# A two-layer hybrid mixer: another opening of the first layer, and three changes to its planner

## Chip, cores and metric

The kernel runs on one core of a Trainium2 chip. The metric is the device time of one execution in microseconds (us). Times of engines and transfers come from one profiled execution.

## What is computed

Two layers, each a modulated RMSNorm, one projection into four token mixers, gates, and an output projection with a residual. There are 512 tokens and 256 context tokens of 1024 channels. Of the reference, this is what the change touches:

```python
def rmsnorm(x, gain):
    xf = x.astype(jnp.float32)
    y = xf * lax.rsqrt(jnp.mean(xf * xf, axis=-1, keepdims=True) + EPS)
    return (y * gain.astype(jnp.float32)).astype(x.dtype)
...
        shift, scale, gate = jnp.split((silu_c @ w_mod[l] + b_mod[l])[:, None, :], 3, axis=-1)
        shift_c, scale_c, gate_c = jnp.split(silu_cc @ w_mod[l] + b_mod[l], 3)
        h = rmsnorm(x, norm_gain[l]) * (1.0 + scale) + shift
        hc = rmsnorm(xc, norm_gain[l]) * (1.0 + scale_c) + shift_c
        za, zb, zh, zf, zg = jnp.split(h @ w_in[l], SPLIT_IDX, axis=-1)
```

## The kernel before

The kernel is written as calls on a recording object, `Program`. `record` (line 199) turns each call into an operation with a cost and a rank; `order` (line 255) then plans all five engines with these costs and fixes one order of instructions for each engine and for the transfer queue of SP. Among the operations that an engine could start at the same planned time, the one of lowest rank comes first. The rank is the place in the program, less `AHEAD` = 400 for the loads and the splitting of weights. On the chip each engine takes its instructions strictly in that order, and each waits on semaphores for what it needs.

Every large product is made of three: an operand is split into a rounded part and a rest, `hi` and `lo` (`split`, line 485: ScalarE, called ACT, rounds; VectorE, called DVE, subtracts), and TensorE, called PE, adds hi·hi, hi·lo and lo·hi in PSUM. Weights arrive as raw blocks `wraw` of 128 x 1024 through SP's queue and are split into `wh` and `wl` in two halves of 512 (`Weights`, line 490). Working tiles are taken from 29 shared slots of 128 x 768, all named `u` in the profile; a tile that takes over a slot waits for the last reader of the one before it.

The stage in question is `opening` (line 653), ahead of the first projection. It loads the 768 tokens as eight blocks `x[j, u]` (3 x 128 tokens, 256 channels each); squares each block on ACT, sums the squares on DVE, and computes the reciprocal root `r` by a chain of small DVE operations (`rstd`, line 744, and `rsqrt`, line 468), once for each half `u` of the tokens; multiplies the blocks by `r` on DVE; transposes them on PE, six blocks of 128 x 128 for each of the eight channel groups `k`, and evicts the result with ACT as `xT[k]`. Meanwhile eight modulation weight chunks arrive, 1 MB each; PE multiplies each with the conditioning (`mod_rows`, tile `psg<-u,cst`), ACT evicts the row (`mrow`), PE turns it into columns (`columns`, `psg<-kc,mrow`) and DVE puts two of them together as scale and shift (`mod_columns`, tile `modc`). Of eight chunks, two are needed for each pair of channel groups. Then

```python
for c, n0, n1 in ((0, 0, NX), (1, NX, NT)):
    ts(xT[k][:, n0:n1], xT[k][:, n0:n1], mc[:, 0, k, c:c + 1], mc[:, 1, k, c:c + 1])
split(hi_t[:, k, :], lo_t[:, k, :], xT[k])
```

makes `h_hi` and `h_lo`, and the first projection (`psw<-h_hi,wh`, the forget gates of the recurrent mixer) starts accumulating as the channel groups come.

The masks of the recurrent mixer are loaded as int32 into slots and cast to int8 on DVE (`load_masks`, called in `hg_mix`).

Of the kernel before, what the change touches and what calls it, by code (L numbers as in the profile page):

```python
# [163 lines left out]
WINDOW = 300  # L164
AHEAD = 400
BEHIND = 0
ATOM = 4
LAT = {"tensor": 0.2, "vector": 0.13, "scalar": 0.15, "gpsimd": 0.13}


class Program:
# [27 lines left out]
    def record(self, engine, method, args, kw):  # L199
        writes = [v for v in [args[0], kw.get("accum_out")] if isinstance(v, View)]  # L200
        reads = [v for v in list(args[1:]) + [v for k, v in kw.items() if k != "accum_out"] if isinstance(v, View)]
        dma = method == "dma_start"
        last = self.last
        if engine == "tensor" and last is not None and last.engine == "tensor" and last.tiles[0] is args[0].tile:
            op = last
        else:
            op = Op(len(self.ops), engine)
            op.rank -= self.ahead
            self.ops.append(op)
        self.last = op  # L210
        op.calls.append((engine, method, args, kw))
        for v in writes + reads:
            if v.tile not in op.tiles:
                op.tiles.append(v.tile)
                v.tile.touch += 1
        for v, w in [(v, False) for v in reads] + [(v, True) for v in writes]:
            r = v.region()
            log = v.tile.log
            for q, x, xw in log:
                if (w or xw) and x is not op and _overlap(r, q):  # L220
                    op.preds.add(x)
            if w:
                log[:] = [e for e in log if not _covers(r, e[0])]
            log.append((r, op, w))
        op.cost += self.price(engine, method, args, kw)
        op.latency = 2.0 if dma else LAT[engine]
        if dma:
            op.transfer = math.prod(args[0].shape) * 4 / 3e5

    def price(self, engine, method, args, kw):  # L230
        o = args[0]
# [23 lines left out]
    def order(self):  # L255
# [15 lines left out]
        for t in span:  # L271
            k = t.space, t.tag
            if k not in free:
                free[k] = [0.0] * t.bufs
                assert live[k].max() <= t.bufs, (k, live[k].max(), int(live[k].argmax()))
        made, done, out, moved = set(), set(), [], 0.0
        oldest = 0
        while len(out) < len(ops):
            while oldest < len(ops) and ops[oldest] in done:
# [78 lines left out]
def tile_hybrid_mixers(ctx, tc, io, out, dump=None):  # L358
# [65 lines left out]
    csel = kc[:, KC_SEL:KC_SEL + 2]  # L424
    rsel = [kc[:, KC_SEL + 2 + w:KC_SEL + 3 + w].to_broadcast([P, P]) for w in range(2)]
    masks = cpool.tile([P, len(LEVELS), P], I8, name="masks")

    hi_t = hpool.tile([P, 8, NT], F32R, tag="hhi", name="h_hi")
    lo_t = hpool.tile([P, 8, NT], F32R, tag="hlo", name="h_lo")

    def load_masks():
        for a, b in ((0, 4), (4, len(LEVELS))):
            mraw = slot([P, b - a, P], I32)
            nc.gpsimd.dma_start(mraw, io["masks"][:, a:b, :])
            nc.vector.tensor_copy(masks[:, a:b, :], mraw)


    sides, done, flags = [], set(), set()
# [53 lines left out]
    class Weights:  # L492
# [3 lines left out]
        def __init__(self, plan):  # L496
            self.plan = list(plan)
            self.raw, self.ready, self.work = [], [], None
            self.held = self.current = 0

        def fetch(self):
            while self.plan and len(self.raw) + bool(self.work) < RAW_BUFS:
                t = wpool.tile([P, 1024], F32, tag="wraw", bufs=RAW_BUFS, name=nm("wraw"))
                nc.ahead = AHEAD
                nc.sync.dma_start(t, self.plan.pop(0))
                nc.ahead = 0
                self.raw.append(t)

        def emit(self):
            if self.work is None:  # L510
                hi, lo = (wpool.tile([P, 1024], F32R, tag=g, bufs=W_BUFS, name=nm(g)) for g in ("wh", "wl"))
                self.work = [hi, lo, self.raw.pop(0), 0]
            hi, lo, raw, a = self.work
            c = slice(a, a + 512)
            nc.ahead = AHEAD
            split(hi[:, c], lo[:, c], raw[:, c])
            nc.ahead = 0
            self.work[3] += 512
            if a + 512 == 1024:
                self.ready.append((hi, lo))  # L520
                self.work = None
                self.fetch()
# [114 lines left out]
        act(rows, ps)  # L637
        return rows

    def columns(tmp, j, rows):  # L640
        ps = psg()[:, 0:4]
        for b in range(2):
            mm(ps[:, 2 * b:2 * b + 2], rows[:, P * b:P * (b + 1)], csel)
        nc.vector.tensor_copy(tmp[:, j // 4, 2 * (j % 4):2 * (j % 4) + 2, :], ps.rearrange("p (k w) -> p k w", w=2))
# [10 lines left out]
    def opening():  # L655
# [3 lines left out]
        tmp = small(32, "mt", 1).rearrange("p (a k w) -> p a k w", a=2, w=2)  # L659
        norm = Norm(None)  # L660
        x = {}
        for u in range(2):
            for j in range(4):
                x[j, u] = slot([P, 3, 256])
                nc.sync.dma_start(x[j, u], io["xin"][384 * u:384 * (u + 1), 256 * j:256 * (j + 1)].rearrange("(t p) d -> p t d", p=P))
        fetch = lambda i: [mod_fetch(io["w_mod"][0, j]) for j in (4 + i, i)]
        w = {0: fetch(0)}
        weights.fetch()
        for u in range(2):
            for j in range(4):  # L670
                sq = slot([P, 3, 256])
                act(sq, x[j, u], AF.Square)
                nc.vector.tensor_reduce(norm.ss[:, 3 * u:3 * u + 3, j], sq, AX.X, ALU.add)
            r = norm.rstd(3 * u, 3 * u + 3, 4)
            for j in range(4):
                tt(x[j, u], x[j, u], r.unsqueeze(2).to_broadcast([P, 3, 256]), ALU.mult)
        w[1] = fetch(1)
        xT = []
        for i in range(4):
            for k in (2 * i, 2 * i + 1):  # L680
                ps = psw()[:, 0:NT]
                for t in range(6):
                    transpose(ps[:, P * t:P * (t + 1)], x[i, t // 3][:, t % 3, P * (k % 2):P * (k % 2 + 1)])
                xT.append(slot())
                act(xT[k], ps)
        for i in range(4):
            for j, wj in zip((4 + i, i), w.pop(i)):
                columns(tmp, j, mod_rows(wj))
            mod_columns(0, mc, tmp, 2 * i, 2 * i + 2)
            for k in (2 * i, 2 * i + 1):  # L690
                for c, n0, n1 in ((0, 0, NX), (1, NX, NT)):
                    ts(xT[k][:, n0:n1], xT[k][:, n0:n1], mc[:, 0, k, c:c + 1], mc[:, 1, k, c:c + 1])
                split(hi_t[:, k, :], lo_t[:, k, :], xT[k])
            if i < 2:
                w[i + 2] = fetch(i + 2)
                for _ in range(4):
                    weights.pump()

    def modulation(l):

# [32 lines left out]
    class Norm:  # L733
# [8 lines left out]
            act(junk, x, AF.Square, accum_out=self.ss[:, t, j:j + 1])  # L742

        def rstd(self, t0, t1, n):
            v = small(3, "sv", 1)
            m = t1 - t0
            nc.vector.tensor_reduce(v[:, 0:m], self.ss[:, t0:t1, 0:n], AX.X, ALU.add)
            ts(v[:, 0:m], v[:, 0:m], 1.0 / D, EPS)
            return rsqrt(v[:, 0:m], m, 3)

        def scale(self, t0, t1, n):

# [505 lines left out]
    def hg_mix(l, z, res):  # L1258
# [1 line left out]
        W = NT if full else NX  # L1260
        nch = W // P
        yield from wait_for((l, "hf", 0))
        if full:
            load_masks()
        fl, om, dl = hg_bounds(l)
        gn = small(64, "hgn", 1)
        nc.gpsimd.dma_start(gn, io["smalls"][l:l + 1, SM_HGG:SM_HGG + 64].partition_broadcast(P).rearrange("p a d -> p (a d)"))
# [345 lines left out]
def _constants():  # L1613
# [13 lines left out]
            kc[r, KC_SEL + w] = 1.0  # L1627
            kc[r, KC_SEL + 2 + w] = 0.5
    i = np.arange(P)
    masks = np.zeros((P, len(LEVELS), P), np.int32)  # L1630
    for n, L in enumerate(LEVELS):
        same = (i[:, None] // (2 * L)) == (i[None, :] // (2 * L))
        masks[:, n] = same & ((i[:, None] // L) != (i[None, :] // L))
# [85 lines left out]
```

## Time and profile before

| what | value |
|---|---|
| median of 3 runs | 1495.21 us (1494.02 to 1495.75) |
| the profiled execution's own time | 1493.43 us |
| its span, first to last instruction | 1491.7 us |
| PE, DVE, ACT busy | 1436.5, 950.8, 627.6 us |

The span leaves 1.7 us of the profiled execution's own time outside. Matmuls overlap, so a row's duration for PE is longer than the step from one to the next, and a busy PE need not be at its peak.

### The profile page before, as it was taken

What the parts mean: (1) busy time and instruction counts of PE and PEld (TensorE: products, weight loads), DVE (VectorE), ACT (ScalarE), POOL (GpSimd) and SP (SyncE); (2) the same over time, 40 slices, a digit from 0 to 9 for tenths busy, and PEclk for the clock granted to TensorE, in tenths of its full rate; (3) what the DMA queues carried; (4) which work ended last, traced back from release to release, by engine and by line L of the source; (5) the groups of instructions that cost most, each with busy time, mean ns of one, the idle gap of its engine ahead of it and who ended that gap; (6) DMA issues with size and microseconds to landing.
All of it is one profiled execution on the core that took longest, in us unless ns stands there. A gap on an engine that the chain in (4) does not pass through costs nothing.

```text
span 1491.7 us, 25385 instructions
## 1 busy us (share of the span) xinstructions
PE 1436.5 (96%) x10068; PEld 1317.4 (88%) x10068; DVE 950.8 (64%) x2058; ACT 627.6 (42%) x1384; POOL 107.2 (7%) x207
## 2 busy tenths in 40 slices
PE   1999999999999999999999999999999999999998
PEld 0899989999999999999999989898888889888788
DVE  5696898677663267633444477889867755674544
ACT  3444353465532245422323354535456633543330
POOL 0000000500000000100000110000130000110000
PEclk9999999999999999999999999999999999999999
DMA  9311101622321135543123321101353222464322
GB/s 349 103 44 57 33 30 60 138 70 97 107 89 57 57 82 169 140 132 123 57 78 101 96 98 57 57 33 58 90 143 88 89 74 88 141 160 160 104 96 78
DMA packets 50598, 144.76 MB, mean 97 GB/s; under 512 B 7280, under 2 KB 12400, under 8 KB 50480
## 3 DMA queue, kind: packets, MB, share of 16 engines
q1 hardware_dynamic: 38336, 112.21, 23.1%
q0 software_dynamic: 12144, 30.93, 8.4%
q8 instruction: 79, 1.29, 0.4%
q14 instruction: 39, 0.32, 0.1%
HBM read 123.98 MB, written 4.19 MB: 86 GB/s over the span
## 4 chain that ended last, share of the span: by engine, by line
PE 86%; DVE 5%; ACT 4%; issue 2%; DMA 2%; SPq 1%; POOL 0%; ACTq 0%; DVEq 0%; POOLq 0%
PE psg L353 70%; PE psw L353 11%; PE pst L353 5%; DVE u L353 4%; ACT u L353 3%; ACT wh L353 1%; DMA u<-u 1%; SPq L353 1%; DVE sm L353 1%; DMA u<-in_w_mod_dram 1%; ACT mth L353 0%; DVE wl L353 0%; DVE nss L353 0%; DVE dd L353 0%; DVE h_lo L353 0%
## 5 line engine op out<-in xcount | busy, mean ns | idle before, releaser
L353 PE MATMUL psg<-h_hi,wh 128*128 128x384 f32 (+2 forms) x1216 | 438.5, 361 | 2.9 <-ACT mth L353 2.8
L353 PE MATMUL psg<-h_hi,wl 128*128 128x384 f32 (+2 forms) x1216 | 428.6, 352 | 0.0
L353 PE MATMUL psg<-h_lo,wh 128*128 128x384 f32 (+2 forms) x1216 | 428.0, 352 | 0.3 <-DVE h_lo L353 0.3
L353 DVE TENSOR_TENSOR wl<-wraw,wh 128x512 fp32r<-128x512 f32 x312 | 201.6, 687 | 186.1 <-ACT wh L353 185.4
L353 ACT ACTIVATE wh<-wraw 128x512 fp32r<-128x512 f32 x312 | 180.6, 625 | 259.3 <-PE psg L353 246.5
L353 PEld LDWEIGHTS psg<-h_hi,wh 128*128 128x128 f32 x1216 | 228.7, 188 | 23.7 <-ACT mth L353 5.7
L353 PEld LDWEIGHTS psg<-h_hi,wl 128*128 128x128 f32 x1216 | 228.5, 188 | 16.0
L353 PEld LDWEIGHTS psg<-h_lo,wh 128*128 128x128 f32 x1216 | 228.9, 188 | 14.5 <-DVE h_lo L353 0.5
L353 PE MATMUL psg<-wh,h_hi 128*128 128x256 f32 x544 | 157.1, 289 | 0.0
L353 PE MATMUL psg<-wl,h_hi 128*128 128x256 f32 x544 | 151.6, 279 | 0.0
L353 PE MATMUL psg<-wh,h_lo 128*128 128x256 f32 x544 | 151.5, 279 | 0.0
L353 PE MATMUL psw<-u,u 64*128 64x128 f32 (+6 forms) x1144 | 135.4, 295 | 8.8 <-ACT u L353 3.1
L353 PEld LDWEIGHTS psw<-u,u 64*128 64x128 f32 (+2 forms) x1144 | 110.8, 188 | 22.0 <-issue 6.0
L353 ACT ACTIVATE u<-psw,sm 128x768 f32<-128x768 f32 (+2 forms) x120 | 90.7, 758 | 77.6 <-DVE sm L353 75.1
L353 DVE SCALAR_TENSOR_TENSOR mth<-mth,psg 128x384 f32<-128x384 f32 (+1 forms) x96 | 57.1, 594 | 87.3 <-ACT mth L353 72.9
L353 ACT ACTIVATE u<-psw 128x768 f32<-128x768 f32 (+10 forms) x208 | 93.8, 472 | 44.2 <-PE psw L353 40.9
L353 PE MATMUL psg<-wh,u 128*128 128x256 f32 x640 | 110.6, 277 | 0.9 <-ACT mth L353 0.9
L353 ACT ACTIVATE mth<-psg 128x384 f32<-128x384 f32 (+1 forms) x120 | 62.3, 520 | 113.2 <-PE psg L353 112.9
L353 PE MATMUL psg<-yg,wh 128*128 128x384 f32 (+1 forms) x384 | 107.1, 360 | 0.0
L353 PEld LDWEIGHTS psg<-wh,h_hi 128*128 128x128 f32 x544 | 102.2, 188 | 3.8
L353 PEld LDWEIGHTS psg<-wl,h_hi 128*128 128x128 f32 x544 | 103.0, 189 | 0.2
L353 PEld LDWEIGHTS psg<-wh,h_lo 128*128 128x128 f32 x544 | 102.3, 188 | 0.0
(134 smaller groups left out, 1960.1 us busy)
## 6 DMA issues: line engine op xcount, KB each, us to landing
wraw<-in_w_merge_dram SPq DMA_DIRECT2D x64, 512.0 KB, 3.5
wraw<-in_w_in_dram SPq DMA_DIRECT2D x60, 512.0 KB, 3.8
u<-in_w_mod_dram SPq DMA_DIRECT2D x32, 384.0 KB, 6.4
wraw<-in_w_up_dram SPq DMA_DIRECT2D x16, 512.0 KB, 3.5
wraw<-in_w_out_dram SPq DMA_DIRECT2D x16, 512.0 KB, 3.8
u<-u POOLq DMA_DIRECT2D x72, 96.0 KB, 2.4
u<-in_w_gate_dram SPq DMA_DIRECT2D x16, 384.0 KB, 6.3
u<-u POOLq DMA_DIRECT2D x24, 192.0 KB, 2.8
```

The costliest lines, as they stand in the source:

```text
L353: getattr(getattr(nc, engine), method)(*map(f, args), **{k: f(v) for k, v in kw.items()})
```

## The change

In `opening`, the token blocks are loaded channel group by channel group, and transposed and evicted unscaled. One chain of roots serves all 768 tokens. Its result is put on the diagonals of six blocks (`dg`) and multiplied by a matrix of ones, so that PE writes `r` as a row over all partitions, evicted as `R`. Then `h = xT * scale * R` is one two-tensor operation on DVE per range of tokens, ACT adds the shift while it rounds (`h_hi`), and a second two-tensor operation on DVE makes `h_lo`. The columns of the modulation use the PSUM buffer `t` in place of one of the three buffers `g`.

The first raw weight blocks lose their early rank during the opening (`rush`). The masks come as int8 straight to their place. In the planner, transfers are costed at 380 bytes per ns in place of 300 and begin at 3.0 us, and an operation other than on PE that reads PSUM has a rank lower by 500.

```diff
+EVICT = 500
...
         dma = method == "dma_start"
+        evict = not dma and engine != "tensor" and any(v.tile.space == "ps" for v in reads)
...
-            op.rank -= self.ahead
+            op.rank -= EVICT if evict else self.ahead
...
-            op.transfer = math.prod(args[0].shape) * 4 / 3e5
+            op.transfer = math.prod(args[0].shape) * 4 / 3.8e5
...
-        made, done, out, moved = set(), set(), [], 0.0
+        made, done, out, moved = set(), set(), [], 3.0
...
+    nc.gpsimd.dma_start(masks, io["masks"])
...
-    def load_masks():
-        for a, b in ((0, 4), (4, len(LEVELS))):
-            mraw = slot([P, b - a, P], I32)
-            nc.gpsimd.dma_start(mraw, io["masks"][:, a:b, :])
-            nc.vector.tensor_copy(masks[:, a:b, :], mraw)
...
-                nc.ahead = AHEAD
+                nc.ahead = self.rush
...
-        for u in range(2):
-            for j in range(4):
+        for j in range(4):
+            for u in range(2):
                 x[j, u] = slot([P, 3, 256])
                 nc.sync.dma_start(x[j, u], io["xin"][384 * u:384 * (u + 1), 256 * j:256 * (j + 1)].rearrange("(t p) d -> p t d", p=P))
...
         weights.fetch()
-        for u in range(2):
-            for j in range(4):
+        w[1] = fetch(1)
+        for j in range(4):
+            for u in range(2):
                 sq = slot([P, 3, 256])
                 act(sq, x[j, u], AF.Square)
                 nc.vector.tensor_reduce(norm.ss[:, 3 * u:3 * u + 3, j], sq, AX.X, ALU.add)
-            r = norm.rstd(3 * u, 3 * u + 3, 4)
-            for j in range(4):
-                tt(x[j, u], x[j, u], r.unsqueeze(2).to_broadcast([P, 3, 256]), ALU.mult)
...
+        for k in range(6):
+            turn(k)
+        r = norm.rstd(0, 6, 4)
+        dg, ones, R = slot([P, 6, P]), slot([P, P]), slot()
+        nc.vector.memset(ones, 1.0)
+        tt(dg, ident.unsqueeze(1).to_broadcast([P, 6, P]), r.unsqueeze(2).to_broadcast([P, 6, P]), ALU.mult)
+        ps = psw()
+        mm(ps[:, 0:512], ones, dg[:, 0:4, :])
+        mm(ps[:, 512:768], ones, dg[:, 4:6, :])
+        act(R, ps[:, 0:NT])
+        for k in (6, 7):
+            turn(k)
...
-                columns(tmp, j, mod_rows(wj))
+                columns(tmp, j, mod_rows(wj), pst()[:, 0:4])
...
-                    ts(xT[k][:, n0:n1], xT[k][:, n0:n1], mc[:, 0, k, c:c + 1], mc[:, 1, k, c:c + 1])
-                split(hi_t[:, k, :], lo_t[:, k, :], xT[k])
+                    h, hi, lo = xT[k][:, n0:n1], hi_t[:, k, n0:n1], lo_t[:, k, n0:n1]
+                    stt(h, h, mc[:, 0, k, c:c + 1], R[:, n0:n1], ALU.mult, ALU.mult)
+                    act(hi, h, AF.Identity, bias=mc[:, 1, k, c:c + 1])
+                    stt(lo, h, mc[:, 1, k, c:c + 1], hi.bitcast(F32), ALU.add, ALU.subtract)
...
+        weights.rush = AHEAD
```

The new `turn(k)` holds the six transposes and the eviction that stood in a loop before. `rstd` and `rsqrt` work on six columns in place of three.

The first place where the order moves is ACT in the opening. Names: `u_176<-u_99` is a square of a token block, `u_305<-psw_290` the eviction of a transposed channel group, `mrow` a modulation row, `wh` the rounding of a raw weight block. Before:

```order
L353 ACTIVATE u_176<-u_99 128x768
L353 ACTIVATE u_185<-u_101 128x768
L353 ACTIVATE u_198<-u_105 128x768
L353 ACTIVATE u_208<-u_107 128x768
L353 ACTIVATE u_228<-u_111 128x768
L353 ACTIVATE mrow_234<-psg_218 128x256
L353 ACTIVATE wh_242<-wraw_131 128x512 x2
L353 ACTIVATE mrow_280<-psg_262 128x256
L353 ACTIVATE u_305<-psw_290 128x768
```

Now:

```order
L355 ACTIVATE u_222<-u_101 128x768
L355 ACTIVATE u_231<-psw_212 128x768
L355 ACTIVATE u_234<-u_103 128x768
L355 ACTIVATE u_246<-psw_224 128x768
L355 ACTIVATE mrow_259<-psg_236 128x256
L355 ACTIVATE u_261<-psw_248 128x768
L355 ACTIVATE u_266<-u_107 128x768
L355 ACTIVATE mrow_282<-psg_268 128x256
L355 ACTIVATE wh_69<-wraw_68 128x512 x2
L355 ACTIVATE wh_297<-wraw_128 128x512 x2
L355 ACTIVATE mrow_341<-psg_323 128x256
L355 ACTIVATE u_359<-psw_346 128x768
```

All eight evictions now stand among the squares; the last square is `u_266<-u_107`. The first two raw blocks (`wraw_68`, `wraw_128`), which stood ahead of the first square, follow it, and `u_359<-psw_346` is the eviction of `R`.

The second place is DVE at the end of the chain of roots (before: the second of two chains). Before:

```order
L353 SCALAR_TENSOR_TENSOR sm_283<-sm_259,sm_277 128x3
L353 TENSOR_TENSOR u_101<-u_101,sm_283 128x768
L353 TENSOR_TENSOR u_105<-u_105,sm_283 128x768
L353 TENSOR_TENSOR u_107<-u_107,sm_283 128x768
L353 TENSOR_TENSOR u_111<-u_111,sm_283 128x768
L353 COPY sm_244<-psg_286 128x4
L353 TENSOR_TENSOR sm_244<-sm_244,cols 128x2x4
L353 SCALAR_TENSOR_TENSOR modc_329<-sm_244,cols 128x4
L353 COPY modc_329<-sm_244 128x4
L353 TENSOR_TENSOR wl_332<-wraw_149,wh_317 128x512 x2
L353 TENSOR_SCALAR u_305<-u_305,modc_329 128x512
```

Now:

```order
L355 SCALAR_TENSOR_TENSOR sm_337<-sm_311,sm_333 128x6
L355 TENSOR_TENSOR u_339<-kc,sm_337 128x768
L355 COPY sm_277<-pst_343 128x4
L355 SCALAR_TENSOR_TENSOR u_164<-u_164,modc_313,u_359 128x512
L355 SCALAR_TENSOR_TENSOR u_164<-u_164,modc_313,u_359 128x256
L355 SCALAR_TENSOR_TENSOR u_168<-u_168,modc_313,u_359 128x512
L355 COPY sm_277<-pst_364 128x4
L355 SCALAR_TENSOR_TENSOR h_lo<-u_164,modc_313,h_hi 128x512
L355 SCALAR_TENSOR_TENSOR h_lo<-u_164,modc_313,h_hi 128x256
L355 SCALAR_TENSOR_TENSOR h_lo<-u_168,modc_313,h_hi 128x512
```

The four scalings of the tokens are gone; one operation builds the diagonals, and the products with `R` (`u_359`) follow. Four halves of `wl`, of the two first raw blocks, stand inside the chain, a little ahead of these rows.

The third place is PE at the start of the first projection (`psw<-h_hi,wh`). Before:

```order
L353 MATMUL psg_377<-u_160,cst 32x256 x2
L353 MATMUL psw_389<-kc,u_99 128x128 x3
L353 MATMUL psw_389<-kc,u_111 128x128 x3
L353 MATMUL psw_397<-kc,u_99 128x128 x3
L353 MATMUL psw_397<-kc,u_111 128x128 x3
L353 MATMUL psw_411<-h_hi,wh_69 128x384
```

Now:

```order
L355 MATMUL psw_346<-u_339,u_81 128x512
L355 MATMUL psw_346<-u_339,u_81 128x256
L355 MATMUL psg_350<-u_143,cst 32x256 x3
L355 MATMUL psg_350<-u_152,cst 32x256 x3
L355 MATMUL psg_350<-u_162,cst 32x256 x2
L355 MATMUL pst_364<-kc,mrow_362 128x2 x2
L355 MATMUL psg_370<-u_166,cst 32x256 x3
L355 MATMUL psg_370<-u_170,cst 32x256 x3
L355 MATMUL psg_370<-u_179,cst 32x256 x2
L355 MATMUL pst_387<-kc,mrow_384 128x2 x2
L355 MATMUL psw_391<-h_hi,wh_69 128x384
```

The transposes stand far ahead now. The spreading of the roots (`psw_346`) and the fourth and fifth modulation rows (`psg_350`, `psg_370`) come last before the projection; before, four rows stood ahead of it.

## Rows read from the trace of the kernel before

**Rows 1.** Windows before and after the first projection's start: busy us of each engine (instructions).
```profile
0.00:47.50 47.50, 17.08 (x124) 11.70 (x124) 29.02 (x72) 19.82 (x31) 5.66 (x14) 1.00 0.94 332
47.50:1491.70 1444.20, 1419.39 (x9944) 1305.74 (x9944) 921.75 (x1987) 607.75 (x1354) 101.58 (x193) 1.00 0.30 89
```

**Rows 2.** Timeline of ACT in the opening: start us, us, engine, line, operation, count, idle before.
```profile
9.13 0.84 ACT L353 ACTIVATE u<-u 128x768 f32<-128x768 f32 x1 [1.07 <-DMA u<-in_xin_dram]
...
21.60 3.78 ACT L353 ACTIVATE u<-u 128x768 f32<-128x768 f32 x5 [7.90 <-PE psg L353]
...
46.68 1.51 ACT L353 ACTIVATE u<-psw 128x768 f32<-128x768 f32 x2 [0.27 <-PE psw L353]
```

**Rows 3.** Timeline of DVE in the opening.
```profile
33.44 1.29 DVE L353 TENSOR_TENSOR wl<-wraw,wh 128x512 fp32r<-128x512 f32 x2
...
36.22 0.36 DVE L353 SCALAR_TENSOR_TENSOR sm<-sm,sm 128x3 f32<-128x3 f32 x2
36.61 3.56 DVE L353 TENSOR_TENSOR u<-u,sm 128x768 f32<-128x768 f32 x4
...
42.41 1.65 DVE L353 TENSOR_SCALAR u<-u,modc 128x512 f32<-128x512 f32 x4
44.31 0.96 DVE L353 TENSOR_TENSOR h_lo<-u,h_hi 128x768 fp32r<-128x768 f32 x1 [0.25 <-ACT h_hi L353]
```

**Rows 4.** Timeline of PE in the opening.
```profile
26.64 1.94 PE L353 MATMUL psg<-u,cst 128*32 128x256 f32 x16
...
37.62 4.41 PE L353 MATMUL psw<-kc,u 128*128 128x128 f32 x21 [6.77 <-DVE u L353]
41.97 1.07 PE L353 MATMUL psg<-u,cst 128*32 128x256 f32 x16
42.97 1.53 PE L353 MATMUL psw<-kc,u 128*128 128x128 f32 x12
...
47.55 0.44 PE L353 MATMUL psw<-h_hi,wh 128*128 128x384 f32 x1 [0.25 <-ACT u L353]
```

**Rows 5.** Windows of 4 us in the opening; the last number is GB/s of all transfers.
```profile
0.00:4.00 4.00, 0.00 (x0) 0.00 (x0) 0.65 (x5) 1.28 (x1) 2.94 (x9) 1.00 0.48 130
4.00:8.00 4.00, 0.00 (x0) 0.00 (x0) 2.07 (x5) 2.35 (x5) 0.06 (x1) 1.00 1.03 360
8.00:12.00 4.00, 0.00 (x0) 0.00 (x0) 1.82 (x3) 1.18 (x3) 0.00 (x0) 1.00 1.04 303
...
24.00:28.00 4.00, 2.31 (x20) 1.53 (x20) 3.68 (x14) 2.68 (x5) 0.00 (x0) 1.00 1.03 400
```

**Rows 6.** Groups in the first 48 us: busy us, mean ns, idle before.
```profile
L353 DVE TENSOR_REDUCE nss<-u 128x3 f32<-128x768 f32 x8 | 7.5, 950 | 10.5 <-ACT u L353 10.5
L353 ACT ACTIVATE u<-u 128x768 f32<-128x768 f32 x8 | 6.3, 836 | 11.0 <-PE psg L353 7.9 <-DMA u<-in_xin_dram 3.1
L353 ACT ACTIVATE u<-psw 128x768 f32<-128x768 f32 x8 | 6.1, 809 | 10.2 <-PE psw L353 10.2
```

**Rows 7.** Groups in the whole span, shapes kept apart.
```profile
L353 PE MATMUL psg<-mrow,kc 128*128 128x256 f32 x24 | 6.5, 378 | 0.0
...
L353 DVE SCALAR_TENSOR_TENSOR mth<-mth,u 128x512 f32<-128x512 f32 x6 | 4.1, 687 | 0.1
L353 DVE SCALAR_TENSOR_TENSOR u<-u,sm,u 128x256 f32<-128x256 f32 x8 | 3.9, 483 | 0.3
```

**Rows 8.** Chain that ended last: start us, us, what.
```profile
70.37 4.16 PE psw L353 x24
```

**Rows 9.** PE's waits after 47.5 us: us in total, times, longest.
```profile
PE psg L353 <- ACT mth L353: 6.6, 14, 0.5
PE psw L353 <- ACT u L353: 5.4, 9, 1.1
```

**Rows 10.** A window in the first layer's mixers, columns as in rows 1.
```profile
165.00:215.00 50.00, 49.77 (x464) 46.75 (x463) 49.14 (x107) 23.84 (x56) 0.00 (x0) 1.00 0.14 43
```

**Rows 11.** ACT's waits in the whole span.
```profile
ACT u L353 <- PE psg L353: 89.7, 53, 7.9
```

More of the change, by code (lines that the diff above doesn't have):

```diff
@@ L499, in __init__ @@
             self.held = self.current = 0
+            self.rush = 0
         def fetch(self):
@@ L514, in emit @@
             c = slice(a, a + 512)
-            nc.ahead = AHEAD
+            nc.ahead = self.rush
             split(hi[:, c], lo[:, c], raw[:, c])
@@ L638, in mod_rows, with columns @@
         return rows
-    def columns(tmp, j, rows):
-        ps = psg()[:, 0:4]
+    def columns(tmp, j, rows, ps=None):
+        ps = psg()[:, 0:4] if ps is None else ps
         for b in range(2):
@@ L673, in opening, with turn @@
                 nc.vector.tensor_reduce(norm.ss[:, 3 * u:3 * u + 3, j], sq, AX.X, ALU.add)
-            r = norm.rstd(3 * u, 3 * u + 3, 4)
-            for j in range(4):
-                tt(x[j, u], x[j, u], r.unsqueeze(2).to_broadcast([P, 3, 256]), ALU.mult)
-        w[1] = fetch(1)
         xT = []
[L679 to L685, printed above, removed]
+        def turn(k):
+            ps = psw()[:, 0:NT]
+            for t in range(6):
+                transpose(ps[:, P * t:P * (t + 1)], x[k // 2, t // 3][:, t % 3, P * (k % 2):P * (k % 2 + 1)])
+            xT.append(slot())
+            act(xT[k], ps)
+        for k in range(6):
[10 more added lines that the diff above has]
+            turn(k)
         for i in range(4):
             for j, wj in zip((4 + i, i), w.pop(i)):
-                columns(tmp, j, mod_rows(wj))
+                columns(tmp, j, mod_rows(wj), pst()[:, 0:4])
             mod_columns(0, mc, tmp, 2 * i, 2 * i + 2)
@@ L744, in rstd @@
         def rstd(self, t0, t1, n):
-            v = small(3, "sv", 1)
             m = t1 - t0
+            v = small(6, "sv", 1)
             nc.vector.tensor_reduce(v[:, 0:m], self.ss[:, t0:t1, 0:n], AX.X, ALU.add)
             ts(v[:, 0:m], v[:, 0:m], 1.0 / D, EPS)
-            return rsqrt(v[:, 0:m], m, 3)
+            return rsqrt(v[:, 0:m], m, 6)
         def scale(self, t0, t1, n):
@@ L1262, in hg_mix @@
         yield from wait_for((l, "hf", 0))
-        if full:
-            load_masks()
         fl, om, dl = hg_bounds(l)
@@ L1629, in _constants @@
     i = np.arange(P)
-    masks = np.zeros((P, len(LEVELS), P), np.int32)
+    masks = np.zeros((P, len(LEVELS), P), np.int8)
     for n, L in enumerate(LEVELS):
```

## The prediction, made before the changed kernel ran

> **What bounds the kernel now.** I read the windows first. Up to 47.5 us PE is busy for 17.1 us; from then on it is busy for 1419.4 of 1444.2 us, idle for 24.8 [rows 1]. So PE bounds all but the opening, and the opening is where time lies. The timelines tell what fills it. ACT squares three token blocks as they land and then stands still for 7.9 us until PE releases a slot; the other five squares run only from 21.60 us [rows 2]. Each of the two chains of roots ends in four scalings of 3.56 us, the second in those at 36.61 us, and PE, idle for 6.77 us because of them, starts most of its transposes at 37.62 us [rows 3, 4]. The first projection starts at 47.55 us, when the evictions of the last transposes end [rows 2, 4]. From there it is a queue of work on PE.
>
> One thing more is to be seen in PE's rows. The windows give a granted clock of 1.00 all along [rows 1, 5], yet a modulation row takes 1.94 us at 26.64 us and 1.07 us at 41.97, and a transpose 0.21 us (4.41 for 21) and then 0.13 (1.53 for 12) [rows 4]. The pace shows the lower and then the higher of the two levels, 1.2 and 2.4 GHz. Before the rise PE had stood idle and then worked from 37.62 us on.
>
> **The change, step by step: when does the projection start?**
>
> Transfers. The tokens, 8 blocks of 0.39 MB, now stand first on SP's queue; two raw weight blocks (1.05 MB) go behind the first two modulation chunks, and the masks shrink by 0.34 MB on POOL's queue. Tokens and constants are 3.5 MB. The opening moved 0.52, 1.44 and 1.21 MB in its first three stretches of 4 us [rows 5], so the last token block lands near 13 us. After that 400 GB/s [rows 5] bring 1.05 MB of modulation in 2.6 us: two chunks by 18.3 us, the two raw blocks by 20.9, a further chunk every 2.6 us.
>
> ACT. From the first block, near 5 us (an estimate: 0.5 MB at these rates), it has eight squares of 0.84, eight evictions of 0.81 [rows 6] and one row of about 0.4: 13.6 us, to 18.6. I add 2 us of waits: PE transposes a group in 1.3 us at its lower pace, and the seventh square takes over the slot of the first modulation piece, which lands only after the tokens. So 20.6 us. Before, the last square ended at 25.4 (five in 3.78 us from 21.60) [rows 2].
>
> DVE. The last sum takes 0.95 [rows 6]. Then stand in its queue thirteen steps of the root chain and five small ones for `modc`, 0.19 each (0.36 for two that overlap) [rows 3], which is 3.4; four halves of `wl`, 1.29 for two [rows 3], which is 2.6 and was done before the tokens landed until now; and the diagonals, 0.9 like one scaling [rows 3]. With 0.5 for ACT's rounding of the raw blocks ahead of `wl` this gives 20.6 + 0.95 + 3.4 + 2.6 + 0.9 + 0.5 = 29.0 us. The 7.1 us of scalings are gone from this path and count here alone.
>
> Spreading. No row shows a product of ones with 768 columns. The nearest are the gate products, 6.5 us for 12 calls of 256 columns (two records each) [rows 7]: 0.54 a call, three times that is 1.6 at the higher pace, 2.9 at the lower (by 1.94 to 1.07). I take 2.2, and the eviction 0.81: 32.0 us.
>
> First groups. Before the first six products can end, DVE must do three products with `R`, a copy and three rests, by the nearest two-tensor rows 0.69 at 512 and 0.48 at 256 [rows 7]: 2 x (0.69 + 0.48 + 0.69) + 0.16 = 3.9, to 35.9. The copy waits for the fourth modulation row, which PE can only start after the spreading, at 31.2; with 1.94 for it, 0.4 for its eviction and nearly 0.9 for its columns that costs 0.9 more. **The projection starts at 36.8 us, 10.8 earlier.**
>
> What then remains. PE has three modulation rows left in place of four: 1.1 less. On DVE a pair of channel groups now costs 2 x (2 x 0.69 + 2 x 0.48) = 4.7 in place of 1.65 + 2 x 0.96 = 3.6 [rows 3, 7]; with its small operations and its part of `wl` about 6.3, against some 5.5 on PE (4.16 for 24 products [rows 8], a row and its columns). DVE can fall behind by 0.8 in each of three pairs; PE's order mixes pairs, so I add 1.0 (bounds 0 and 2.4). Casts (0.8) and POOL's issues were covered and are worth nothing. Opening in all: 10.8 + 1.1 - 1.0, **10.9 us saved**, with bounds of 7 (transfers and first square 2 later, DVE's lag at its bound) and 14 (PE at its higher pace, a last square without waits).
>
> DVE's products are where a page speaks against the change. The Trainium skill (VectorE: DVE Perf Modes, The perf-mode tier table) says that an fp32 operation with one tensor runs at twice the rate of one with two. By that rule the four products of a pair cost twice the 1.65 us, 3.3, where I have 2.3 by rows; DVE's lag would grow by up to 1 us a pair and the opening save 8 instead of 10.9. The rows that exist speak for the smaller price.
>
> The rest of the program. The new rank of evictions and the new costs of transfers reorder all later work; the work itself stays. PE's waits on ACT after 47.5 us that an earlier eviction could end are 6.6 and 5.4 us [rows 9]. Ending all gives 12; the other bound is a loss, of which below. Most are under half a microsecond each, so I take 2 of the 12.
>
> Sum: 10.9 + 2 = 12.9 us off the profiled execution's 1493.4, thus 1480.5. That execution lies 1.8 below the median, 1495.2; against the median it is **1482 us**.
>
> **Rivals.**
> - More comes out: the opening saves 14 and most of those waits end (8 of 12). 1495.2 - 22 = 1473. For it: the waits are short and of one kind. Against: they add up only if each is cured.
> - PE's lower clock holds into the projection. Its first 24 products then take 1.8 times 4.16, 3.4 more: 1486. For it: the work of 26 to 31 us did not raise the pace, and now PE's early work comes in pieces. Against: from 27 us on it has the spreading and two rows nearly without a break. The Trainium skill (TensorE: Matmul & The Clock Gate, What's actually happening) has the half rate as the default state, released by activity; these rows agree with it.
> - The change does not do what it says: squares still wait for slots, or the raw blocks land late and hold the root chain, as `wl` stands in it. Each microsecond there is one of the start. With 6 us lost: 1488. For it: the stall of 7.9 us before was of this kind. Against: only one square waits so now.
> - The gain is taken back where DVE is full, 49.1 of 50 us between 165 and 215 us [rows 10], if PE comes there earlier and DVE does not: 1494. Against: DVE's work there is started by the same projections, which come earlier too.
> - **Slower.** An eviction ranked first stands at the head of a strict queue; where PE is later than planned, ready work behind it waits. ACT's waits of that kind are 89.7 us in 53 times now, 1.7 each [rows 11]. It decides in the mixers, where DVE has under 1 us to spare in 50 [rows 10] and waits for ACT's results: eight such waits more there cancel the 13 us, and twelve give 1495.2 - 13 + 20 = 1502. Against: PE is nearly always the one that others wait for, so its own work goes on.
>
> **How the numbers follow.** About 0.2%, 3 us, can be told from no change. The chances: forecast 0.50, more comes out 0.12, lower clock 0.10, change not as said 0.13, gain taken back 0.07, slower 0.08. The first four are faster: 0.85; same 0.07; slower 0.08. The range goes from 1473 to 1491: its lower end is the rival with more gain, and its upper takes in the opening's bound of 7 without any gain later (1488) and 3 us lost to the new order. It leaves out the two last cases and a little of the tails, 0.2 in all.
>
> **What would show it.** In the timeline after: squares without a long pause, the last ending near 20.6 us; the diagonals near 29 and the eviction of `R` ending near 32; the first product of the projection near 36.8, with modulation rows at 1.94 or 1.07 telling the clock. In the windows PE's idle after that start should be 22 to 25 us. A start near 37 with a time above 1490 would mean that the new order lost it; a start after 42 that the opening is not what I worked out.

## The result, and the profile after

The changed kernel takes **1479.21 us** (median of 4 runs, 1477.64 to 1481.64) against 1494.62 of the kernel before on the same chip: a ratio of 0.9898, 95% interval 0.9886 to 0.991, or 15.4 us less. The forecast was 1482 us, range 1473 to 1491. The profiled execution took 1477.64 us, 15.8 less than that of before; its span is 1475.9 us. That execution is the fastest of the four.

The windows, cut at the new start of the projection, answer to [rows 1] (columns as there):

```profile
0.00:33.20 33.20, 20.65 (x152) 13.51 (x153) 18.14 (x48) 20.43 (x31) 5.12 (x13) 0.94 0.97 342
33.20:1475.90 1442.70, 1420.88 (x9921) 1310.45 (x9921) 925.55 (x1998) 610.75 (x1362) 101.29 (x193) 1.00 0.30 92
```

The projection starts at 33.21 us, 14.3 earlier than at 47.55 [rows 4]. After that PE is idle for 21.8 us, where it was 24.8, and busy 1.5 longer: 14.3 + 3.0 - 1.5 = 15.8. So in this execution nearly all of the gain is in the opening. ACT's timeline there answers to [rows 2]:

```profile
5.78 1.56 ACT L355 ACTIVATE u<-u 128x768 f32<-128x768 f32 x2
...
9.10 0.81 ACT L355 ACTIVATE u<-psw 128x768 f32<-128x768 f32 x1 [0.40 <-PE psw L355]
...
19.31 0.86 ACT L355 ACTIVATE u<-u 128x768 f32<-128x768 f32 x1
...
28.67 0.81 ACT L355 ACTIVATE u<-psw 128x768 f32<-128x768 f32 x1 [2.09 <-PE psw L355]
```

The stall of 7.9 us is gone. Squares and evictions alternate, and the last square ends at 20.17 us. DVE's timeline answers to [rows 3]:

```profile
20.21 0.95 DVE L355 TENSOR_REDUCE nss<-u 128x3 f32<-128x768 f32 x1 [0.61 <-ACT u L355]
...
22.26 0.16 DVE L355 TENSOR_SCALAR sm<-sm 128x6 int32<-128x6 int32 x1
22.33 0.68 DVE L355 TENSOR_TENSOR wl<-wraw,wh 128x512 fp32r<-128x512 f32 x1
...
25.97 0.96 DVE L355 TENSOR_TENSOR u<-kc,sm 128x768 f32<-128x768 f32 x1
...
29.51 1.81 DVE L355 SCALAR_TENSOR_TENSOR u<-u,modc,u 128x512 f32<-128x512 f32 x3 [2.08 <-ACT u L355]
```

A step of the root chain (22.26) takes 0.16 by itself, but the half of `wl` behind it starts 0.07 later: between halves of `wl` a step is nearly free. The diagonals end at 26.93 us, and DVE then waits for `R`. PE, answering to [rows 4]:

```profile
7.52 7.00 PE L355 MATMUL psw<-kc,u 128*128 128x128 f32 x36 [7.52 <-DMA kc<-in_consts_dram]
...
27.10 1.54 PE L355 MATMUL psw<-u,u 128*128 128x512 f32 x4
28.56 1.07 PE L355 MATMUL psg<-u,cst 128*32 128x256 f32 x16
...
32.55 0.80 PE L355 MATMUL pst<-kc,mrow 128*128 128x2 f32 x4 [0.54 <-ACT mrow L355]
33.21 0.67 PE L355 MATMUL psw<-h_hi,wh 128*128 128x384 f32 x1
33.68 0.52 PE L355 MATMUL psw<-h_lo,wh 128*128 128x384 f32 x1
34.00 0.52 PE L355 MATMUL psw<-h_hi,wl 128*128 128x384 f32 x1
```

The first products follow each other in steps of 0.32 us; from 36 us on the step is 0.17. Here the windows of 4 us show the lower level for part of the time (the third number from the end, 1.00 all along in [rows 5]):

```profile
24.00:28.00 4.00, 3.47 (x19) 1.49 (x17) 2.85 (x11) 0.38 (x1) 0.54 (x1) 0.75 1.04 394
...
32.00:36.00 4.00, 3.46 (x20) 2.78 (x22) 4.00 (x13) 2.20 (x5) 0.00 (x0) 0.60 1.03 392
```

PE's waits after the start answer to [rows 9]:

```profile
PE psw L355 <- ACT sq L355: 6.3, 1, 6.3
...
PE psw L355 <- ACT u L355: 4.1, 7, 1.1
```

The 14 waits for `mth`, 6.6 us, are gone. One wait of 6.3 us is new, which the view puts down to a square (`sq`); it lies at the boundary between the layers:

```profile
870.27 6.74 PE L355 MATMUL psw<-u,u 128*128 128x128 f32 x32 [6.31 <-ACT sq L355]
```

These products read a token block and the diagonals of its roots, which DVE writes:

```profile
869.84 0.48 DVE L355 TENSOR_SCALAR u<-kc,sm 128x128 f32<-128x128 f32 x2
```

The first of these two ends at 870.12 us, 0.15 before PE goes on; in the kernel before it ends at 884.14, 0.14 before the products at 884.28. So it is the diagonals that PE waits for; the square, of a later block, happens to end at the same time. Below, "the wait on a square" is the name that the view gives.

Before, the same products came in two pieces:

```profile
884.28 2.02 PE L353 MATMUL psw<-u,u 128*128 128x128 f32 x16 [0.90 <-DVE u L353]
888.75 2.02 PE L353 MATMUL psw<-u,u 128*128 128x128 f32 x16 [2.44 <-issue]
```

So the rest of the program is not unchanged: something was gained and something lost. To see where, I numbered the 6912 products that read `wh` or `wl` in the order of their starts and took, for every 120th, its start in one trace less the start of the product of the same number in the kernel before. The columns are places by the time in the kernel before; small differences near a place can come from another order. Each row is one execution.

| kernel | 155 | 400 | 822 | 912 | 1480 us |
|---|---|---|---|---|---|
| changed | -14.6 | -15.2 | -21.3 | -12.2 | -16.1 |
| 1 no rank | -15.7 | -15.4 | -15.5 | -15.5 | -15.4 |
| 2 old transfer costs | -14.9 | -14.3 | -20.1 | -11.6 | -15.4 |
| 3 opening alone | -11.6 | -11.0 | -11.2 | -9.8 | -10.0 |
| 4 planner alone | -0.8 | -1.4 | -7.8 | -1.2 | -6.4 |
| 5 rank for tanh | -18.3 | -18.3 | -21.3 | -21.3 | -23.1 |
| 6 place plain | -11.7 | -12.3 | -18.4 | -12.5 | -15.7 |
| 7 chain first | -13.4 | -14.0 | -19.4 | -13.1 | -15.6 |
| 8 raw blocks first | -10.3 | -10.5 | -15.9 | -7.3 | -11.2 |
| 9 transfer costs alone | 3.1 | -0.1 | -0.2 | 1.2 | 1.2 |
| 10 old opening, tanh | 3.7 | 2.4 | -0.7 | -0.7 | -2.7 |
| 11 fillers | -18.6 | -18.5 | -21.1 | -21.1 | -22.8 |
| 12 boundary plain | -13.9 | -14.5 | -20.6 | -17.1 | -20.4 |

The changed kernel gains 15 us in the opening and 6 more up to the boundary, loses 9 there and gains 4 in the second layer.

About 2 of these 9 us are no wait. In the output projection (`psg<-wh,u` and `psg<-wl,u`, 960 products of 256 columns) PE starts a product every 117.7 ns in the changed kernel and every 113.3 in the kernel before, at a granted clock of 1.00 in both. Two thirds of them, before and now:

```profile
L353 PE MATMUL psg<-wh,u 128*128 128x256 f32 x640 | 110.6, 277 | 0.9 <-ACT mth L353 0.9
```

```profile
L355 PE MATMUL psg<-wh,u 128*128 128x256 f32 x640 | 114.6, 282 | 0.0
```

That is 960 x 4.4 ns = 4.2 us, 2.5 in the first layer (2.1 of it behind the place at 822 us) and 1.7 in the second. Runs 2, 6, 7, 8 and 12 have the slower step too, the others (1, 3, 4, 5, 9, 10, 11) the faster, with both kinds on the same chips. So it comes with the new opening and the low rank of all evictions together, and with neither alone; why is not shown.

### The profile page after: what moved, and what is told of

Same layout as the page of the kernel before. It is cut to its first block, busy times and chain, and to the rows that moved or that the text cites. A ratio compares the mean times of both kernels' runs of the same rounds, so it can differ in the third digit from the quotient of the medians.

```text
span 1475.9 us, 25322 instructions
## 1 busy us (share of the span) xinstructions
PE 1441.5 (98%) x10072; PEld 1324.0 (90%) x10072; DVE 943.7 (64%) x2045; ACT 631.2 (43%) x1393; POOL 106.4 (7%) x206
## 4 chain that ended last, share of the span: by engine, by line
PE 88%; DVE 6%; ACT 3%; DMA 1%; issue 1%; SPq 0%; DVEq 0%; ACTq 0%
PE psg L355 71%; PE psw L355 11%; PE pst L355 5%; DVE u L355 5%; ACT u L355 2%; DMA u<-in_w_mod_dram 1%; DVE wl L355 1%; DVE sm L355 0%; SPq L355 0%; ACT h_hi L355 0%; ACT wh L355 0%; DVE h_lo L355 0%; DVE dd L355 0%; DVE gu L355 0%; DVE ou L355 0%
## 5 line engine op out<-in xcount | busy, mean ns | idle before, releaser
L355 PEld LDWEIGHTS psg<-h_hi,wh 128*128 128x128 f32 x1216 | 228.7, 188 | 20.6 <-ACT mth L355 2.5
L355 PEld LDWEIGHTS psg<-h_hi,wl 128*128 128x128 f32 x1216 | 228.5, 188 | 15.9
L355 PEld LDWEIGHTS psg<-h_lo,wh 128*128 128x128 f32 x1216 | 229.0, 188 | 14.6 <-DVE h_lo L355 0.5
L355 PE MATMUL psw<-u,u 64*128 64x128 f32 (+7 forms) x1148 | 137.9, 297 | 13.2 <-ACT sq L355 6.3
L355 PE MATMUL psg<-wh,u 128*128 128x256 f32 x640 | 114.6, 282 | 0.0
```

The source lines that it names most:

```text
L355: getattr(getattr(nc, engine), method)(*map(f, args), **{k: f(v) for k, v in kw.items()})
```

## Experiments

The first four take the change apart. **1, the lower rank taken away:**

```diff
-            op.rank -= EVICT if evict else self.ahead
+            op.rank -= self.ahead
```

> The changed kernel, but reads of PSUM get no lower rank; everything else as changed. The theory (the opening brought 14.3 us of start and 1.6 us of a modulation row, and the first rank of evictions saves PE's short waits on the evictions mth, 6.6 us, and costs as much at the layer boundary, where PE waits once for 6.3 us on a square): start of the projection within 1 us of 33.2, the 14 waits on mth (6.6 us) return, the single wait on a square goes, 1476 to 1482 us. The rival (the rank is worth the waits it removed and the boundary is not its doing): the mth waits return, the wait on a square stays, 1484 to 1487 us. A second rival (the rank is a net loss): below 1474 us.

Measured: 1478.34 us, ratio 0.9895 (0.9881 to 0.9909). The waits on `mth` are back and the one on the square is gone:

```profile
PE psg L355 <- ACT mth L355: 6.6, 14, 0.5
```

As the theory had it, but for the start, which came at 28.96 us and not near 33.2. From 155 us on this kernel is 15.5 us ahead without change, so opening and transfer costs together give 15.5. The rank as a whole is worth nothing: it gains some 10 us in two places and loses 9 in one, by the slower products in part.

**2, the old transfer costs** (`3e5` and `0.0` in place of `3.8e5` and `3.0`).

> The changed kernel with the planner's old transfers (300 bytes per ns, from 0 us). The theory: the chip moves transfers as before and PE seldom waits for one after the start, so the plan of the opening shifts by at most 1 us and the time stays at 1477 to 1482 us. The rival: with late planned tokens the planner puts raw blocks and modulation rows elsewhere among the evictions, the start slips by 2 us or more: 1482 to 1486 us.

Measured: 1478.46 us, ratio 0.9894 (0.988 to 0.9907), a time as the theory had it. The plan of the opening did shift, which the theory had at 1 us at most: the projection starts at 29.06 us, 4.2 earlier than in the changed kernel, and yet at 155 us the two stand alike (-14.9 and -14.6). Beside the lower rank the transfer costs matter little in the end.

**3, both undone:** the new opening and the masks alone.

> The new opening and the masks alone, planner as before (no lower rank for reads of PSUM, old transfers). The theory: all of the gain is here, 14 to 16 us less than the kernel before, 1478 to 1482 us. The rival (planner changes bring some 5 us and the opening 10): 1484 to 1487 us.

Measured: 1483.16 us, ratio 0.9924 (0.9911 to 0.9938): 11.8 less, between the two. The projection starts at 30.23 us, earlier than in the changed kernel, and yet the opening is worth only 11. Its windows and PE's timeline show why:

```profile
36.00:40.00 4.00, 4.00 (x26) 2.83 (x25) 0.00 (x0) 0.25 (x1) 0.00 (x0) 0.64 1.05 394
```

```profile
34.17 0.67 PE L355 MATMUL psw<-h_hi,wh 128*128 128x384 f32 x1
...
38.28 1.33 PE L355 MATMUL psg<-u,cst 128*32 128x256 f32 x16
```

Planned as if transfers were slow, the next modulation row stands behind twelve products, which take 4.1 us at PE's lower level, and DVE, which needs the row's columns, does nothing from 36 to 40 us. The start of the projection is not the end of the opening.

**4, the kernel before with the planner's three numbers alone.**

> The kernel before with the planner's three new numbers alone (rank of evictions, 380 bytes per ns, from 3 us); the opening as before. The theory: no gain worth the name, within 4 us of the kernel before, 1491 to 1498 us; the mth waits go and others take their place. The rival (the planner's part is worth 5 us by itself): 1488 to 1490 us. A second rival (in the old opening evictions first delay the squares): the projection starts after 48.5 us and the time is above 1497 us.

Measured: 1486.25 us, ratio 0.9947 (0.9934 to 0.9959): 8.7 less, more than theory or rivals allowed. The table has it: 6.4 gained between 400 and 822 us, 6.6 lost at the boundary, with the same wait of 6.3 us on a square, and 5.2 gained in the second layer. The parts do not add: 11.8 and 8.7 make 20.5, and together they bring 15.4. Of the missing 5.1 us the slower products are 4.2: neither part alone has them.

**5, the lower rank for the tanh evictions alone** (ACT's tanh into `mth`, and DVE's product of `mth` with a PSUM buffer, which is written into the same tile):

```diff
-any(v.tile.space == "ps" for v in reads)
+any(v.tile.space == "ps" for v in reads) and args[0].tile.tag == "mth"
```

> The changed kernel, but the lower rank goes only to the evictions of tanh (mth). The theory (three parts that add: opening with the new transfer costs 15.5 us, as in the run without the rank; the 14 waits on mth 5 to 6 us; the layer boundary costs 7 us only where its evictions are ranked first): no mth waits, no wait on a square, 1472 to 1475 us. The rival (the loss at the boundary comes from any shift of the order before it): the wait on a square is there, 1477 to 1480 us.

Measured: **1471.34 us**, ratio 0.9854 (0.9841 to 0.9868), 22.2 less than before and better than both kernels, and 0.7 below what was expected. No wait on `mth`, none on a square; nothing is lost at the boundary, and the products have the faster step. About half of what the rank gains between 400 and 822 us is lost there again, mostly in a wait for a transfer at 596 us that the changed kernel does not have:

```profile
PE psw L355 <- DMA u<-u: 2.3, 1, 2.3
```

Runs 10 and 11 have it too, with 2.0 and 2.7 us.

**6, plain rank for the evictions in `place`,** which turn the products with the diagonals into `h`:

```diff
+            nc.plain = True
             for g in range(2):
...
+            nc.plain = False
```

where `record` gives the lower rank only without `plain`.

> The changed kernel, but the evictions that make h at the layer boundary (place) keep their plain rank. The theory (there the evictions, ranked first, cut up the chain of roots on DVE, 10.5 us in place of 6.0): the wait of 6.3 us on a square goes, 1470 to 1474 us. The rival (the chain is held by the squares or by the splitting of weights, not by these evictions): the wait stays within 2 us of 6.3, 1476 to 1480 us.

Measured: 1477.65 us, ratio 0.9891 (0.9875 to 0.9906). A wait of 4.8 us for the same products stays; the view now names DVE. These evictions were not the whole cause.

**7, the small steps of the chain of roots ranked as low as the evictions there** (`nc.ahead = EVICT` around `rstd` and the diagonals in `scale`).

> The changed kernel, but at the layer boundary the small steps of the chain of roots get the evictions' low rank too. The theory (it is the chain that matters, not that evictions wait): as in the run with plain evictions there, 1470 to 1474 us, and the chain takes 6 us or less. The rival: the chain's first input, the square, is what is late; the wait stays, 1476 to 1480 us.

Measured: 1478.84 us, ratio 0.9903 (0.9889 to 0.9916), in the rival's range though the 6.3 us wait is gone. The second block's diagonals now come 8.5 us after the first block's transposes begin, as in the kernel before, where it was 13.7 in the changed kernel. The loss moved to the third block. DVE's timeline there:

```profile
868.72 0.42 DVE L355 TENSOR_TENSOR gu<-psg,u 128x256 f32<-128x256 f32 x1
869.05 0.69 DVE L355 TENSOR_TENSOR wl<-wraw,wh 128x512 fp32r<-128x512 f32 x1
869.79 0.41 DVE L355 TENSOR_SCALAR u<-psw,modc 128x128 f32<-128x128 f32 x1
870.73 1.08 DVE L355 TENSOR_SCALAR u<-psw,modc 128x128 f32<-128x128 f32 x3 [0.53 <-ACT u L355]
871.72 1.28 DVE L355 TENSOR_TENSOR wl<-wraw,wh 128x512 fp32r<-128x512 f32 x2
873.55 0.73 DVE L355 TENSOR_SCALAR u<-psw,modc 128x128 f32<-128x128 f32 x2 [0.55 <-ACT u L355]
874.20 0.41 DVE L355 TENSOR_TENSOR u<-u,gu 128x256 f32<-128x256 f32 x1
```

The product with the gate (`gu`, an eviction) is done at 869.1, but the residual sum that the next square reads, a plain operation, runs at 874.20, behind six evictions and the splitting of weights. In run 5 these two start 0.65 us apart, here 5.5. So the rule that evictions come first puts every plain step of the path to the next diagonals behind them.

**12, both kinds of evictions at the boundary plain** (run 6, and `plain` around the product with the gate in the first layer). DVE's order there is then that of run 5.

> The changed kernel, but at the layer boundary both kinds of evictions keep their plain rank: those that make h (place) and the products with the gate (gu) that lead to the next square. The theory (at the boundary the work that leads to the next block's diagonals, which is the products with the gate, the residual sums, squares and the chain of roots, competes on DVE with evictions of the block before; with all of them in program order PE waits there as in the kernel before): no wait over 2.5 us on PE after 840 us, 1470 to 1474 us. The rival (with the low rank elsewhere PE comes to the boundary 5 us earlier and DVE does not): a wait of 4 us or more stays, 1476 to 1479 us.

Measured: 1474.87 us, ratio 0.9873 (0.9856 to 0.9889), 0.9 above what was expected; the longest wait after 840 us is 2.4. The boundary loses 3.5 us in place of 9, and 4.3 us come off the changed kernel. So the stall there is the rank of these two kinds of evictions. The 3.5 that stay are in the trace: 2.1 are the slower products, and 1.4 come from sixteen products that this execution ran at the lower level, 3.46 us where run 5 has 2.02, behind a wait that both have:

```profile
870.26 3.46 PE L356 MATMUL psw<-u,u 128*128 128x128 f32 x16 [2.43 <-issue]
```

**8, raw weight blocks first again** (`self.rush = AHEAD` from the start).

> The changed kernel, but raw weight blocks keep their early rank in the opening, as before. The theory (the opening's end is set by the last modulation chunk, since in every kernel so far the transfers run at about 395 GB/s until some 42 us, and not by the start of the projection): with two raw blocks, 1.05 MB, ahead of the tokens the start slips by up to 2.6 us, but all chunks land as before, and 1477 to 1480 us come out. The rival of the prediction's reckoning (each microsecond of the start is one of the end): 1480.5 to 1484 us.

Measured: 1482.40 us, ratio 0.9926 (0.9914 to 0.9939). The theory fell, and the time is in the rival's range: the first square starts at 9.80 us in place of 5.78, 4.0 later, and at 155 us this kernel stands 4.3 behind the changed one. The projection starts at 39.19 us, not 2.6 but 6.0 later than in the changed kernel's profiled execution, and 3.2 to 4.1 later than in runs 6, 7 and 12, where the spreading ran at the lower level as it did here (2.93 us). Against these, a microsecond of the start is about one of the end. So the early landing of the tokens is worth some 4 us of the change.

**9 and 10, the old opening** with the new transfer costs alone, and with these and the rank for tanh alone.

> The kernel before, with the planner's new transfer costs alone (380 bytes per ns, from 3 us), no lower rank for reads of PSUM, old opening. The theory (with the old opening the new costs change little, and the opening is worth more with them, 16.6 us in place of 11.8): within 2 us of the kernel before, 1492 to 1496 us. The rival (the new costs are worth some 4 us by themselves, whatever the opening): 1488 to 1491 us.

> The kernel before, with the new transfer costs and the lower rank for tanh alone: all of the run of 1471.3 us but its opening and masks. The theory (the opening gives 15 to 18 us of the 22.2, the tanh evictions 5 to 6): 1486.5 to 1490 us. The rival (the parts do not add, since the run with all planner changes and the old opening had 1486.3 us with a stall of 6.3 us in it): 1480 to 1484 us.

Measured: 1494.37 us, ratio 0.9997 (0.9988 to 1.0006), and 1489.99 us, ratio 0.9969 (0.9958 to 0.998). The transfer costs alone are worth nothing; with the new opening and no rank they are worth 4.8 (runs 1 and 3). The rank for tanh gives 4.1 to 5.6 (runs 10; 5 against 1), and run 5 less run 10 leaves some 18 for the new opening and masks.

Runs 4 and 10 both have the old opening and the faster step of products, and differ in which evictions have the low rank. Between 400 and 822 us run 4 gains 6.4 and run 10 gains 3.1, in the second layer 5.2 and 2.0; at the boundary run 4 loses 6.6 and run 10 nothing. So the evictions other than tanh's pay some 6 us away from the boundary (2 of it is run 10's wait for a transfer, which run 4 does not have) and lose as much there. A kernel that takes the first without the second and without the slower products was not run; run 12 is the nearest, with the slower products.

**What differs between equal openings.** Up to the boundary the changed kernel and runs 6, 7 and 12 have the same order on every engine, and so have runs 1 and 5 in the opening. Yet at 155 us they stand at -14.6, -11.7, -13.4, -13.9, and at -15.7 and -18.3. The projection starts at 33.21, 36.03, 35.74 and 35.12 us in the first four: the changed kernel's profiled execution is the early one. It spread `R` in 1.54 us, the other three in 2.91, as run 6 shows:

```profile
28.07 2.91 PE L356 MATMUL psw<-u,u 128*128 128x512 f32 x4
...
36.03 0.67 PE L356 MATMUL psw<-h_hi,wh 128*128 128x384 f32 x1
```

PE's timelines of run 1,

```profile
21.15 1.93 PE L355 MATMUL psg<-u,cst 128*32 128x256 f32 x16
23.01 2.68 PE L355 MATMUL psw<-u,u 128*128 128x512 f32 x4
...
28.96 0.45 PE L355 MATMUL psw<-h_hi,wh 128*128 128x384 f32 x1 [1.28 <-ACT h_hi L355]
```

and of run 5,

```profile
20.46 1.07 PE L355 MATMUL psg<-u,cst 128*32 128x256 f32 x16
21.46 1.56 PE L355 MATMUL psw<-u,u 128*128 128x512 f32 x4
...
26.29 0.45 PE L355 MATMUL psw<-h_hi,wh 128*128 128x384 f32 x1 [0.49 <-ACT h_hi L355]
```

with the windows of both, run 1 and run 5:

```profile
20.00:24.00 4.00, 4.00 (x24) 2.22 (x23) 0.94 (x2) 1.64 (x3) 0.00 (x0) 0.50 1.03 400
```

```profile
20.00:24.00 4.00, 4.00 (x39) 2.81 (x40) 1.93 (x5) 2.55 (x5) 0.00 (x0) 1.00 1.03 400
```

Of the same work, one execution has a stretch at 1.2 GHz where the other has 2.4, and that makes 2.7 us of the start and 2.6 at 155 us. **11** tried to hold the level: run 5 with four more transposes ahead of each channel group's six (overwritten) and eight of `R` into a tile that nobody reads.

> The kernel with the rank for tanh alone, with fillers on PE in the opening that the planner counts at nothing: four transposes more ahead of each channel group's six, whose results are overwritten, and eight of R into a tile that nobody reads; 40 instructions, 5.8 us of PE at its pace in the higher level. The order of all else stays. The theory (two runs with the same opening started 2.7 us apart because PE worked at its lower level from 18 to 25 us in one of them; a PE that stands idle less keeps the higher one): spreading in 1.6 us and rows in 1.1, the granted clock at 1.00 from 16 to 30 us, 1468 to 1471 us. The rival (the fillers delay the evictions and the modulation rows, and the level falls anyway when PE waits for DVE): rows at 1.9 us again, 1472 to 1475 us.

Measured: 1470.95 us, ratio 0.9845 (0.9827 to 0.9863). In its profile the granted clock is 1.00 from 6 to 46 us, rows take 1.07 and the spreading 1.56; its projection starts 1.3 us later than run 5's (27.57 against 26.29), and at 155 us it stands 0.3 ahead. But run 5 had drawn the higher level for the spreading too, and its times (1470.3 to 1473.2 against 1469.1 to 1474.1) cannot be told from these. Whether fillers hold the level in every execution stays open.

## Why the prediction was right, step by step

**The bound** was read rightly: PE after the start, and the opening ahead of it.

**The start** was forecast at 36.8 us and came at 33.2, in one execution; the three others of the same order (runs 6, 7, 12) started at 35.1 to 36.0. Last square: 20.6 forecast, 20.2 measured. Diagonals: 29.0 forecast, 26.9 measured, and 27.1 to 27.7 in the three others; this is the mis-sized term. I had added 18 small steps at 0.19 to four halves of `wl`; from 21.16 to 26.93 lie 5.8 us, less 0.96 for the diagonals and 4 x 0.68 for the halves makes 2.1 for steps and rounding, where I had 3.4 + 0.5. Steps between other work of the same engine start 0.07 us ahead of it, as at 22.26. Spreading: 1.54 us, close to the bound of 1.6 that I had given for the higher level, not 2.2; in run 6 it took 2.91, the other bound. Both bounds were right, and which one comes is a matter of the execution. First groups: 3.7 in place of 4.8, since the fourth row ran at 1.07 and not 1.94; the last thing ahead of the first product is not DVE but the columns of PE's fifth row, at 32.55. Together 0.4 + 1.7 + 0.4 + 1.1 = 3.6 us. Only the diagonals were wrong in every execution; the last 1.5 us are mostly the clock that this one drew. One sum was off by itself: 31.2 + 1.94 + 0.4 + 0.9 for the fourth row's columns is 34.4, which is 0.6 and not 0.9 behind the three products that end at 33.9, so these terms give a start of 36.5.

**DVE's two-tensor products** were priced at 0.69 and 0.48 us by the nearest rows. The groups of the changed kernel in the first 60 us, and those of the one-tensor operations in the kernel before:

```profile
L355 DVE SCALAR_TENSOR_TENSOR u<-u,modc,u 128x512 f32<-128x512 f32 x8 | 5.9, 737 | 2.1 <-ACT u L355 2.1
...
L355 DVE SCALAR_TENSOR_TENSOR u<-u,modc,u 128x256 f32<-128x256 f32 x8 | 3.8, 479 | 0.0
```

```profile
L353 DVE TENSOR_SCALAR u<-u,modc 128x512 f32<-128x512 f32 x6 | 3.3, 544 | 0.1
L353 DVE TENSOR_SCALAR u<-u,modc 128x256 f32<-128x256 f32 x6 | 2.5, 409 | 0.0
```

Four products of a pair cost 2 x (0.737 + 0.479) = 2.4 us; I had 2.3. The Trainium skill (VectorE: DVE Perf Modes, The perf-mode tier table) has twice the rate for one tensor. The rows of this case agree for each further element, (737 - 479) / 256 = 1.01 ns against (544 - 409) / 256 = 0.53, but not for the whole instruction, which at 512 elements is only 1.35 times as long. By the Trainium skill's sentence I had 3.3 us for the four; the rows decide. PE waits once on DVE from the start to 100 us, 0.8 us at 76.6, in the mixers, where the kernel before has a like wait of 0.9 at 96.0; so the lag of 1.0 in the opening that I had added did not come.

**The rest of the program.** From the start on I had 1.1 - 1.0 + 2 = 2.1 us less, and 1.5 came. That is near, but not for the reason given: the step that failed is "most are under half a microsecond each, so I take 2 of the 12". The rank ended all 6.6 us of the waits for `mth` and made a stall at the boundary, and "the work itself stays" put at nothing the step of 960 products, which cost 4.2 us more. The sum held because gains and losses nearly cancel, which is luck; and with the start at 35.1 to 36.0, as in the other executions, the opening alone gives 11.5 to 12.4 and not 14.3.

**The rivals.** The lower clock came in part: six first products at 0.32 in place of 0.17 us cost 0.9, and between equal orders the level makes up to 2.7. "Slower" had the right mechanism, ready work behind a ranked eviction in a strict queue, at the wrong place and price: not in the mixers and not on ACT alone, but in DVE's path of the boundary, one wait of 6.3 us and then 32 products at a granted clock of 0.58, in 6.74 us where 2 x 2.02 stood. "More comes out" is what run 5 is: with the rank for tanh alone, 22 us, the size given there, though by other parts: 18 from opening and masks with the new transfer costs, and 4 to 6 from the waits. No square waited for a slot longer than 0.2 us, and the table shows nothing taken back between 155 and 400 us. PE's idle after the start was 21.8 us, just under the 22 to 25 that were to show the forecast.

## What to carry to other kernels

A blanket rule of rank in a planner (all evictions first) should be tried by class and by place: the class whose waits the trace shows, here tanh, paid 4 to 6 us by itself; the others paid some 4 to 6 more away from the boundary, but at the boundary they put plain steps of a serial path behind ready bulk work, and lost as much. Compare also the step from product to product where nothing waits: here it moved by 4% with the order and took 4.2 us. Price small steps on an engine by what stands between them, not by their own duration. Take the start of a stage from more than one execution: with one order it lay anywhere between 33.2 and 36.0 us. And where the first product starts says less than when the last input of a stage is ready: run 3 started 3 us before the changed kernel and came out of the opening 3 us behind it.

## What the runs showed of the hardware

Equal orders of instructions draw different levels of TensorE's clock in the opening, with up to 2.8 us between their starts. The Trainium skill (TensorE: Matmul & The Clock Gate, What's actually happening) has the half rate as the default, released by activity; the first 18 transposes of run 5 take 4.10 us, 0.23 each, and later groups of six 0.88, 0.15 each, which agrees.

A granted clock of 1.00 in these windows need not mean the full pace. Runs 9 and 10 in the opening, the same window:

```profile
28.00:32.00 4.00, 3.47 (x32) 1.75 (x28) 3.90 (x7) 0.39 (x1) 0.00 (x0) 1.00 1.03 401
```

```profile
28.00:32.00 4.00, 3.47 (x32) 1.78 (x28) 3.90 (x8) 0.38 (x1) 0.00 (x0) 0.50 1.03 399
```

One is granted 1.00 and the other 0.50, and both do the same 32 matmuls in 3.47 us, a modulation row at 27.4 in 1.93 us in both. The column alone does not tell the pace, and neither does a row's duration, which holds short pauses too. This row of run 5 takes 1.85 us:

```profile
23.94 1.85 PE L355 MATMUL psg<-u,cst 128*32 128x256 f32 x16
```

Yet each of its matmuls takes 0.38 to 0.40 us, as in rows of 1.07, and not 0.63, as in those of 1.93: it ran at the higher level with gaps in between. The duration of the single matmul tells the pace.
